# A fused attention and expert layer: the last products before routing in halves of the tokens, indexer heads in pairs, idle products, and a bank for each last quarter

## The chip, the cores and the metric

The kernel runs on one core of a Trainium2 chip. The metric is the device time of one execution in microseconds. The core has TensorE (PE, its weight loads listed apart as PEld), VectorE (DVE), ScalarE (ACT), GpSimd (POOL) and SyncE (SP), which here issues all transfers. Matrix products go to PSUM, eight banks of 128 x 512 float32; VectorE and ScalarE read them from there.

## The reference, cut to what matters

One layer on 256 tokens of width 1024, all float32:

```python
h = rmsnorm(x, g); proj = h @ w_in                     # split into latents, q/k/v, indexer q/k/w, two gates
y_a = attention(latents)  @ w_o_a                      # 8 heads, chunk-causal
score = sum_h w_i[h] * relu(q_i[h] @ k_i.T)            # indexer: 8 heads of 64, one key head
sel = top_k(score, 64)                                 # per query; attention B reads these keys alone
y_b = sparse_attention(q_b, k_b, v_b, sel) @ w_o_b
x = x + (sigmoid(g_a) * y_a + sigmoid(g_b) * y_b) @ w_out
h2 = rmsnorm(x, g2)
g_sel = argmax(h2 @ w_router_group); top 2 of the 4 experts in that group
for e in range(32):                                    # d_ff 256
    out += (silu(h2 @ w_gate[e]) * (h2 @ w_up[e])) @ w_down[e] * combine[:, e]
return rmsnorm(x + out, g_fin)
```

## The kernel before

The 256 tokens are two halves t = 0, 1 of 128. All weights stream from memory in slabs of 128 x 2048 float32 (1 MB) through SyncE's queue into a ring of 22 places; a slab's transfer is issued when the last reader of its place is done (`may_issue`, `issue`, `take`). Slabs of attention weights come first; the 96 slabs of expert weights (`w_moe`, three per expert in all: two for gate and up, and one per expert's worth of down) follow into every place that the attention stage gives up. The last three are transferred in two halves each. Places S0 and S1 hold the split parts of the last attention slabs.

Front. Products that need accuracy are done as three fp32r matmuls of high and low parts (`mm3`, lines 301 to 303: high by high, high by low, low by high). ScalarE makes the high part, VectorE the low one. Nearly all of the front is ordered by the framework's planner, which simulates a timeline. `select(j)` computes the indexer's scores for query half j: 8 heads, each a product of 64 rows (heads 0 to 3 lie in partitions 0 to 63, heads 4 to 7 in 64 to 127) with 128 key columns for j = 0 and 256 for j = 1, packed to a bank of 512 columns (`pss`, a pool of two banks), then Relu on ScalarE and a weighted sum on VectorE.

Last products. The output projection `w_out` accumulates in four banks, `acc[2*t + h]` for half t of the tokens and half h of the columns. From `raw = take()[1]` (line 872) the order on PE is written out by hand (`manual_schedule`), and from line 887 that on ScalarE and VectorE too. `last_product(t, k)` is one `mm3` of the last four slices k of column half h = 1. `added` adds the residual on VectorE, `squared` sums squares on ScalarE, `turned` transposes four blocks on PE and copies them out (`kept`), `logits` does the router's products on the turned blocks (two groups of four blocks per half of the tokens), `inv_root` makes 1/rms (square root on ScalarE, four steps on VectorE), `chosen(t)` picks group and experts in nine steps on VectorE, `cums` counts places by a product with a triangle, `place_of` and `slots` make a one-hot matrix of token to slot (`P_`) and scale it by 1/rms (`Pr`), and `gather(c, t, p)` gathers tokens for expert group 0 by products with `Pr`. `residual(i)` starts the output sums `OA` from x2 by an identity product. VectorE's work for t = 1 before is: root, choosing, then the placing of half 0, then that of half 1; the four gathers follow as (0,0), (1,0), (0,1), (1,1).

Experts. Eight groups of four experts; a group's tokens (up to 32 slots per expert) are multiplied with gate and up slabs (`gate_up`, line 993, four experts' columns of 32 side by side), folded (`hidden`, line 1009), and then with four down slabs, a quarter of the output columns each (`down`, line 1030: two halves f = 0, 1 of d_ff). `combine` evicts a result with the routing weight as high and low parts (`ysb`, line 297) and scatters it into `OA` by a product (line 1044). In groups 0 to 6 two quarters share a bank and one eviction; in the last group each quarter is evicted alone, but quarters 0 and 1, and 2 and 3, still share a bank `Y`. An engine's access to a bank is ordered behind another engine's access to the same bank, whichever columns they use. `heat(bank, n)` issues n products of 128 x 256 in bfloat16 whose result is not used. In the last group 4 of them follow each gate and up half from the second expert on. `final_part` makes x * g_fin (VectorE) and the sum of squares (ScalarE) of a finished part of the columns: 0 to 511 after quarter 2, 512 to 767 after quarter 3's eviction, and 768 to 1023 after the last scatter (line 1174 on). Then follow the root, the scaling and two output transfers.

## Time and profile before

| | us |
|---|---|
| three runs | 432.21, 435.72, 435.73 (median 435.72) |
| the profiled execution, its own time | 431.72 |
| its span, first to last instruction | 430.0 |
| TensorE busy / VectorE / ScalarE | 397.2 / 206.7 / 184.6 |
| bytes moved | 134.98 MB, 314 GB/s on the mean |

The profile is of one execution, whose time is 1.72 us above its span; it lies near the lowest of the three runs. Times in the trace count from the span's start. A matmul's row has its modelled end, so two rows overlap and the distance between starts is what a matmul takes of PE. A "releaser" (after the arrow) is what ended the idle time before an instruction.

### The profile page before, as it was taken

The page shows a single profiled execution, that of the slowest core. Times are in us where ns is not written, and L with a number is a line of the kernel's source. Part 1 is how long each engine was busy: PE and PEld are TensorE (multiplying, and loading weights), DVE is VectorE, ACT ScalarE, POOL GpSimd, SP SyncE. Part 2 cuts the span into 40 slices and gives each one's busy share as a digit, 9 for nine tenths or more (in the row PEclk, how much of TensorE's full clock was granted, in tenths as well). Part 3 has the DMA queues.
Part 4 walks back from the last instruction along what each step waited for, and adds up shares of the span by engine and source line. Part 5 has one row for each costly group of instructions (what it writes and reads, how often), then busy time and mean ns, then how long its engine had stood idle before and what let it go on. Part 6 is the DMA issues. An engine that isn't in the chain of part 4 may idle for free.

```text
span 430.0 us, 8090 instructions
## 1 busy us (share of the span) xinstructions
PE 397.2 (92%) x3255; PEld 291.6 (68%) x3255; DVE 206.7 (48%) x547; ACT 184.6 (43%) x407; POOL 26.5 (6%) x30
## 2 busy tenths in 40 slices
PE   6999999999999999999989999999999798787760
PEld 3888878888867777888877757575757374364420
DVE  2899599989757464757563221221213011020033
ACT  4885586677756566565433122212221111120242
POOL 0870000000000000000001010101010101000000
PEclk9999999999999999999999999999999979699995
DMA  7985573648543456888994999999999999999952
GB/s 261 390 357 238 196 287 111 257 171 343 197 150 143 148 204 238 325 312 335 332 356 171 425 419 418 422 419 419 420 420 421 419 419 421 421 420 418 414 215 103
DMA packets 20638, 134.98 MB, mean 314 GB/s; under 512 B 2418, under 2 KB 2930, under 8 KB 5620
## 3 DMA queue, kind: packets, MB, share of 16 engines
q1 hardware_dynamic: 20596, 134.42, 79.1%
q8 instruction: 27, 0.44, 0.4%
q14 instruction: 15, 0.12, 0.1%
HBM read 133.36 MB, written 1.05 MB: 313 GB/s over the span
## 4 chain that ended last, share of the span: by engine, by line
PE 70%; DMA 24%; DVE 2%; ACT 1%; issue 0%; SPq 0%; DVEq 0%; ACTq 0%
DMA w<-in_w_moe 23%; PE a L301 13%; PE a L302 13%; PE a L303 12%; PE G L993 8%; PE gx L844 4%; PE Y L1030 3%; PE G L1009 2%; PE OA L1044 2%; PE o L595 2%; PE s L301 2%; PE t L583 1%; PE s L303 1%; PE s L302 1%; DMA w<-in_w_att 1%; PE t L532 1%
## 5 line engine op out<-in xcount | busy, mean ns | idle before, releaser
L302 PE MATMUL a<-r 128*128 128x512 f32 (+1 forms) x244 | 93.7, 388 | 0.0
L303 PE MATMUL a<-r 128*128 128x512 f32 (+1 forms) x244 | 91.9, 383 | 0.0
L301 PE MATMUL a<-r 128*128 128x512 f32 (+1 forms) x244 | 83.7, 387 | 1.0 <-ACT r L297 1.0
L993 PE MATMUL G<-w,tok 128*32 128x256 f32 x1024 | 70.0, 401 | 13.3 <-DMA w<-in_w_moe 13.3
L297 DVE SCALAR_TENSOR_TENSOR r<-w,ident,r 128x512 fp32r<-128x512 f32 (+2 forms) x79 | 62.0, 799 | 13.5 <-ACT r L297 13.3
L297 ACT ACTIVATE r<-w,ident 128x512 fp32r<-128x512 f32 (+2 forms) x79 | 56.6, 751 | 27.4 <-PE a L303 26.2
L993 PEld LDWEIGHTS G<-w,tok 128*32 128x32 f32 x1024 | 29.6, 113 | 39.8 <-issue 15.3
L302 PEld LDWEIGHTS a<-r 128*128 128x128 f32 x244 | 45.9, 188 | 8.6 <-DVE r L297 0.4
L301 PEld LDWEIGHTS a<-r 128*128 128x128 f32 x244 | 44.8, 188 | 10.3 <-ACT r L297 1.9
L303 PEld LDWEIGHTS a<-r 128*128 128x128 f32 x244 | 45.8, 188 | 8.3
L1015 DVE TENSOR_TENSOR P<-G,P 128x64 f32<-128x64 f32 x32 | 7.2, 225 | 82.7 <-ACT P L1014 82.7
L1014 ACT ACTIVATE P<-G 128x64 f32<-128x64 f32 x32 | 7.2, 224 | 75.1 <-PE G L1009 75.1
L1030 PE MATMUL Y<-w,P 128*32 128x256 f32 x512 | 30.5, 382 | 3.2 <-DVE ysb L297 2.2
L999 ACT COPY Gs<-G 128x256 f32<-128x256 f32 x32 | 11.9, 372 | 48.0 <-PE G L993 48.0
L844 PEld LDWEIGHTS gx<-Pr,x 128*128 128x128 f32 x256 | 29.8, 195 | 3.9 <-issue 3.3
L844 PE MATMUL gx<-Pr,x 128*128 128x128 f32 x256 | 31.4, 282 | 0.5 <-DVE Pr L829 0.5
L297 DVE SCALAR_TENSOR_TENSOR ysb<-Y,ws,ysb 128x512 fp32r<-128x512 f32 (+1 forms) x18 | 12.4, 691 | 37.6 <-ACT ysb L297 20.3
L283 DVE TENSOR_TENSOR r<-w,r 128x512 fp32r<-128x512 f32 x32 | 21.9, 690 | 16.7 <-ACT r L282 15.1
L829 POOL TENSOR_SCALAR Pr<-P,r 128x128 f32<-128x128 f32 x14 | 8.3, 607 | 323.5 <-PE gx L844 198.8
L282 ACT CAST r<-w 128x512 fp32r<-128x512 f32 x32 | 19.9, 624 | 14.6 <-PE a L303 9.5
L1030 PEld LDWEIGHTS Y<-w,P 128*32 128x32 f32 x512 | 15.4, 109 | 13.7 <-DVE ysb L297 3.2
L849 DVE TENSOR_TENSOR tok<-gx,ident 128x512 f32<-128x512 f32 x16 | 11.1, 692 | 27.4 <-PE gx L844 27.3
(211 smaller groups left out, 482.2 us busy)
## 6 DMA issues: line engine op xcount, KB each, us to landing
w<-in_w_moe SPq DMA_DIRECT2D x93, 1024.0 KB, 19.8
w<-in_w_att SPq DMA_DIRECT2D x24, 1024.0 KB, 4.9
w<-in_w_moe SPq DMA_DIRECT2D x6, 512.0 KB, 15.0
w<-in_w_att SPq DMA_DIRECT2D x3, 744.0 KB, 8.5
w<-in_w_att SPq DMA_DIRECT2D x2, 512.0 KB, 5.0
out<-r SPq DMA_DIRECT2D x2, 512.0 KB, 3.8
w<-in_w_att SPq DMA_DIRECT2D x1, 768.0 KB, 4.8
w<-in_w_att SPq DMA_DIRECT2D x2, 372.0 KB, 6.1
```

The source lines that it names most:

```text
L282: nc.scalar.copy(hi, src)
L283: nc.vector.tensor_sub(lo, src, hi.bitcast(F32))
L297: return nc.scalar.mul(hi, ps, g), nc.vector.scalar_tensor_tensor(lo, ps, g, hi.bitcast(F32), op0=ALU.mult, op1=ALU.subtract)
L301: i = nc.tensor.matmul(out_, lh, rh, start=start, stop=False)
L302: nc.tensor.matmul(out_, lh, rl, start=False, stop=False)
L303: nc.tensor.matmul(out_, ll, rh, start=False, stop=stop)
L595: nc.tensor.matmul(o[r, c * 256 + 128 * b:(c + 1) * 256], v[:, b, 64 * (4 * quad + h):][:, :64], PT[:, h, 0:2] if b == 0 else PT[:, h, 2], ...
L844: nc.tensor.matmul(p[:, kk * GRP:(kk + 1) * GRP], x2[:, t, k * 128:(k + 1) * 128], Pr[:, t], start=(t == 0 and kk == 0), stop=(t == 1 and ...
L849: nc.vector.tensor_mul(tokens[c], p.rearrange("p (k s) -> p k s", k=4), bc(g_ffn[:, 4 * c:4 * c + 4], GRP, axis=2))
L993: nc.tensor.matmul(G[quarters[2 * z + o], :256], tokens[c][:, kk + o, CAP * e:CAP * e + CAP], w[:, (kk + o) * 512 + z * 256:(kk + o) * 512 ...
L999: nc.scalar.copy(Gs, G[:, :256])
L1030: nc.tensor.matmul(Y[quarters[e]], hT_[:, e, f], wv[:, f, e], start=f == 0, stop=f == 1)
```

## The change

- `select` takes heads h and h + 4 together: `mm3_pair` issues each of the three matmuls of a product for the one head and then for the other, into two banks; then both Relu and the sums follow. The order of the sum over heads changes.
- The eight last products go half by half: all four of t = 0 and then those of t = 1, with the turns and router products of both halves between them. The choosing of half 0 starts before the addition of half 1 and is completed after it. The root of half 1, the placing of half 0 (its scaled slots on POOL) and only then the choosing of half 1 follow on VectorE. Three of the four `residual` products move behind the counts, five idle products follow them, and the last count moves behind the first gather.
- `HEAT` is 5 instead of 4. In the last four `down` quarters 5 idle products stand between the halves f = 0 and f = 1 ahead of the scatter, 2 behind each quarter and 10 ahead of the last scatter.
- Each of the last four quarters has a bank of its own. The final part of columns 512 to 1023 is done in one piece after the last scatter. A scatter takes the high parts for both halves of the tokens and then the low parts, in all groups.

```diff
--- before.py
+++ after.py
@@ -23,7 +23,7 @@
 TAKEN = -3e38
 NG, EPG, NE = 8, 4, 32
 
-HEAT = 4
+HEAT = 5
 CAP = 32
 GRP = EPG * CAP
 TOPK = 64
@@ -308,6 +308,14 @@
         m = ident_r.bitcast(mybir.dt.bfloat16)
         for _ in range(n):
             nc.tensor.matmul(bank[:, 256:], m[:, :128], m, start=True, stop=True)
+
+    row_halves = slice(0, 64), slice(64, 128)
+
+    def mm3_pair(both, start, stop):
+
+        for l, r, s0, s1 in ((1, 3, start, False), (1, 4, False, False), (2, 3, False, stop)):
+            for ops in both:
+                nc.tensor.matmul(ops[0], ops[l], ops[r], start=s0, stop=s1)
 
     scr_turn = [0]
 
@@ -468,19 +476,18 @@
         per = 512 // nk
         qs = slice(j * 128, (j + 1) * 128)
         sc = e0[:, 1664:1920] if j else e0[:, 1536:1664]
-        for h0 in range(0, 8, per):
-            p = pss()
+        for h0 in range(0, 4, per):
+            p = [pss() for _ in range(2)]
             for i in range(per):
-                h = h0 + i
-                ps_ = slice(64 * (h // 4), 64 * (h // 4) + 64)
-                mm3(p[:, i * nk:(i + 1) * nk], qiT[ps_, 0, h % 4, qs], qiT[ps_, 1, h % 4, qs],
-                    kiT[ps_, 0, :nk], kiT[ps_, 1, :nk], True, True)
-            rl = wk.tile([128, 512], F32, tag="b2", name="rl", bufs=3)
-            nc.scalar.activation(rl, p, AF.Relu)
-            for i in range(per):
-                h = h0 + i
-                nc.vector.scalar_tensor_tensor(sc, rl[:, i * nk:(i + 1) * nk], wi[:, j, h:h + 1],
-                                               adm[:, 256 - nk:] if h == 0 else sc, op0=ALU.mult, op1=ALU.add)
+                mm3_pair([(p[z][:, i * nk:(i + 1) * nk], qiT[ps_, 0, h0 + i, qs], qiT[ps_, 1, h0 + i, qs],
+                           kiT[ps_, 0, :nk], kiT[ps_, 1, :nk]) for z, ps_ in enumerate(row_halves)], True, True)
+            for z in range(2):
+                rl = wk.tile([128, 512], F32, tag="b2", name="rl", bufs=3)
+                nc.scalar.activation(rl, p[z], AF.Relu)
+                for i in range(per):
+                    h = 4 * z + h0 + i
+                    nc.vector.scalar_tensor_tensor(sc, rl[:, i * nk:(i + 1) * nk], wi[:, j, h:h + 1],
+                                                   adm[:, 256 - nk:] if h == 0 else sc, op0=ALU.mult, op1=ALU.add)
         for r in range(TOPK // 8):
             m8 = wk.tile([128, 8], F32, tag="m8", name="m8")
             nc.vector.max(out=m8, in_=sc)
@@ -875,24 +882,22 @@
     def last_product(t, k):
         out_product(t, 1, 1, k, *last[k])
 
-    for k in range(2):
+    for k in range(4):
         last_product(0, k)
-        last_product(1, k)
-        turned(0, 4, k, 2)()
+        if k in (1, 2):
+            turned(0, 4, k - 1, 2)()
     logits(0, 4, 0)
-    last_product(0, 2)
-    last_product(0, 3)
+    last_product(1, 0)
     urgent = ctx.enter_context(ExitStack())
     urgent.enter_context(tc.high_priority(300))
     urgent.enter_context(tc.manual_schedule(engines={mybir.EngineType.Activation, mybir.EngineType.DVE}))
     added(512, 512, 0, acc[1])
     squared(512, 512, 0, 1)
     early = [early_root(ss2[:, t, 0:1], D, f"n2{t}") for t in range(2)]
-    last_product(1, 2)
-    last_product(1, 3)
+    last_product(1, 1)
     kept = turned(4, 4, 0, 4)
     logits(0, 4, 1)
-    added(512, 512, 1, acc[3])
+    last_product(1, 2)
     kept()
 
     def in_turn(*chains):
@@ -902,25 +907,33 @@
             chains = [c for c in chains if next(c, chains) is not chains]
 
     in_turn(inv_root(ss2[:, 0, 1:2], D, "n20", early[0], r2[:, 0:1], True))
+    logits(4, 4, 0)
+    last_product(1, 3)
+    chain = chosen(0)
+    next(chain)
+    next(chain)
+    added(512, 512, 1, acc[3])
     squared(512, 512, 1, 1)
     kept = turned(4, 4, 1, 4)
-    logits(4, 4, 0)
+    in_turn(chain)
     kept()
     cums = [pt("cum") for _ in range(2)]
-    in_turn(inv_root(ss2[:, 1, 1:2], D, "n21", early[1], r2[:, 1:2], True), chosen(0))
+
+    residual(0)
     logits(4, 4, 1)
-
-    residual(0)
-    residual(1)
     nc.tensor.matmul(cums[0][:, :NE], tri, sel[:, 0], start=True, stop=True)
     nc.tensor.matmul(cums[1][:, :NE], ones, sel[:, 0], start=True, stop=False)
+    residual(1)
     residual(2)
     residual(3)
+    heat(lgp[0], 5)
+    in_turn(inv_root(ss2[:, 1, 1:2], D, "n21", early[1], r2[:, 1:2], True))
+    place_of(0, cums[0][:, :NE])
+    in_turn(slots(0, 0, nc.gpsimd))
     in_turn(chosen(1))
-    in_turn(placed(0, cums[0][:, :NE]))
     gx = [pss("gx") for _ in range(2)]
+    gather(0, 0, gx[0])
     nc.tensor.matmul(cums[1][:, :NE], tri, sel[:, 1], start=False, stop=True)
-    gather(0, 0, gx[0])
     gather(1, 0, gx[1])
     in_turn(placed(1, cums[1][:, :NE]))
     gather(0, 1, gx[0])
@@ -1021,9 +1034,13 @@
 
     def down(grp, q, w, between=None):
 
-        if q % 2 == 0:
-            Ys[grp, q // 2] = pss("Y")
-        Y = Ys[grp, q // 2][:, 256 * (q % 2):256 * (q % 2) + 256]
+        if q % 2 == 0 or grp == NG - 1:
+            bank = pss("Y")
+            Ys[grp, q] = bank[:, :256]
+            if grp < NG - 1:
+                Ys[grp, q] = bank
+                Ys[grp, q + 1] = bank[:, 256:]
+        Y = Ys[grp, q][:, :256]
         wv = w.rearrange("p (f e c) -> p f e c", f=2, e=EPG)
         for f in range(2):
             for e in range(EPG):
@@ -1036,11 +1053,11 @@
         h, c0, w = q0 // 2, 256 * (q0 % 2), 256 * n
         pl, ws = pls[grp]
         hi, lo = (wk.tile([128, 512], F32R, tag="b2", name="ysb", bufs=3)[:, :w] for _ in range(2))
-        evac_g(hi, lo, Ys[grp, h][:, c0:c0 + w], ws)
+        evac_g(hi, lo, Ys[grp, q0][:, :w], ws)
 
         def scatter():
-            for t in range(2):
-                for v in (hi, lo):
+            for v in (hi, lo):
+                for t in range(2):
                     nc.tensor.matmul(OA[t][h][:, c0:c0 + w], pl[:, t * 128:(t + 1) * 128], v, start=False,
                                      stop=grp == NG - 1 and q0 > 0 and v is lo,
                                      skip_group_check=grp == NG - 1 and q0 == 3)
@@ -1154,29 +1171,33 @@
                 if q % 2:
                     todo.append(combine(grp, q - 1, 2))
 
-        scatter = None
+        def between():
+            heat(idle_bank, HEAT)
+            if scatter:
+                scatter()
+
+        scatter, idle_bank = None, pt("heat")
         for q in range(4):
-            down(grp, q, take()[1], scatter)
+            down(grp, q, take()[1], between)
+            heat(idle_bank, 2)
             scatter = combine(grp, q, 1)
             if q == 2:
                 for t in range(2):
                     final_part(t, 0, 512, 0)
             elif q == 3:
-                for t in range(2):
-                    final_part(t, 512, 256, 1)
-                nc.vector.tensor_add(fs[:, :, 0], fs[:, :, 0], fs[:, :, 1])
                 early = [early_root(fs[:, t, 0:1], D, f"nf{t}") for t in range(2)]
+        heat(idle_bank, 2 * HEAT)
         scatter()
 
 
     rf = sm([128, 2], "rf")
     with tc.manual_schedule(engines={mybir.EngineType.Activation, mybir.EngineType.DVE}):
-        cs = slice(768, 1024)
-        for t in range(2):
-            nc.vector.tensor_mul(ob[:, t, cs], OA[t][1][:, 256:], g_fin[0][:, cs])
+        cs = slice(512, 1024)
+        for t in range(2):
+            nc.vector.tensor_mul(ob[:, t, cs], OA[t][1], g_fin[0][:, cs])
         roots = []
         for t in range(2):
-            sumsq(OA[t][1][:, 256:], 256, fs[:, t, 2:3], scr[:, 2 * t + 1, 256:])
+            sumsq(OA[t][1], 512, fs[:, t, 2:3], scr[:, 2 * t + 1])
             roots.append(inv_root(fs[:, t, 2:3], D, f"nf{t}", early[t], rf[:, t:t + 1], True))
         for t in range(2):
             in_turn(roots[t])
```

## Rows read from the trace of the kernel before

**Rows 1.** The page: the granted clock of TensorE in 40 slices of the span, in tenths of full speed (9 is 90% or more), and from the chain that ended last its shares by engine.

```profile
PEclk9999999999999999999999999999999979699995
PE 70%; DMA 24%; DVE 2%; ACT 1%; issue 0%; SPq 0%; DVEq 0%; ACTq 0%
```

**Rows 2.** The windows view: stretch, its length, busy us (and count) of PE, PEld, DVE, ACT, POOL, then granted clock, share of the transfer engines, GB/s.

```profile
75.00:115.00 40.00, 40.00 (x229) 33.47 (x228) 36.01 (x104) 28.20 (x65) 0.00 (x0) 1.00 0.63 236
...
224.00:228.00 4.00, 3.05 (x25) 2.64 (x24) 2.98 (x21) 1.10 (x6) 0.18 (x1) 1.00 0.21 84
...
236.00:408.00 172.00, 158.44 (x1904) 102.62 (x1896) 30.68 (x87) 30.95 (x83) 7.13 (x12) 0.96 1.01 420
```

**Rows 3.** The timeline of SyncE's queue: start, duration, issues of slab transfers. No other issue lies between these two rows.

```profile
217.95 0.81 SPq L215 DMA_DIRECT2D w<-in_w_moe  x2
...
230.56 1.19 SPq L215 DMA_DIRECT2D w<-in_w_moe  x2
```

**Rows 4.** The timeline of PE in `select`: start, duration, line, result and operands, rows*columns of the weights and the moving operand's shape, count.

```profile
59.59 0.33 PE L301 MATMUL s<-r 64*128 64x128 f32 x2
...
60.21 0.27 PE L303 MATMUL s<-r 64*128 64x128 f32 x1
60.32 0.27 PE L301 MATMUL s<-r 64*128 64x128 f32 x1
...
66.19 0.28 PE L303 MATMUL s<-r 64*128 64x256 f32 x1
66.31 0.28 PE L301 MATMUL s<-r 64*128 64x256 f32 x1
```

**Rows 5.** The timeline of the last products: the first matmul of the first of the eight and the next one, the addition for half 0, and the last matmul of the last of the eight. At the end two rows of the chain that ended last (start, us on the chain): a turn and eight router products.

```profile
210.47 0.39 PE L301 MATMUL a<-r 128*128 128x512 f32 x1
...
210.69 0.39 PE L302 MATMUL a<-r 128*128 128x512 f32 x1
...
216.58 0.69 DVE L751 TENSOR_TENSOR x<-a,x 128x512 f32<-128x512 f32 x1 [1.46 <-PE a L303]
...
217.52 0.40 PE L303 MATMUL a<-r 128*128 128x512 f32 x1
...
217.92 0.44 PE t L761 x4
218.36 0.82 PE s L778 x8
```

**Rows 6.** The timeline of the routing: copy of turned blocks, two residual products, choosing for half 1 (its first step), the placing of half 0 (place, and 0.70 us later, behind the slots, the scaled slots), the four gathers, a scaling on POOL, the first expert products.

```profile
219.69 0.58 ACT L769 COPY x2T<-t 128x512 f32<-128x512 f32 x1
...
222.57 0.25 DVE L792 SCALAR_TENSOR_TENSOR lg<-s,r,b_r 128x40 f32<-128x40 f32 x1
...
223.20 1.11 PE L859 MATMUL OA<-x,ident 128*128 128x256 f32 x4
...
224.63 0.18 DVE L821 SCALAR_TENSOR_TENSOR place<-cum,sel 128x32 f32<-128x32 f32 x1
...
225.33 0.28 DVE L829 TENSOR_SCALAR Pr<-P,r 128x128 f32<-128x128 f32 x1
...
225.66 3.84 PE L844 MATMUL gx<-Pr,x 128*128 128x128 f32 x32 [0.48 <-DVE Pr L829]
...
227.82 0.61 POOL L829 TENSOR_SCALAR Pr<-P,r 128x128 f32<-128x128 f32 x1 [197.63 <-PE gx L844]
...
229.43 2.80 PE L993 MATMUL G<-w,tok 128*32 128x256 f32 x48
```

**Rows 7.** The tail. First the last slab's second half: its issue in the queue's timeline, and the transfers view of it (KB, us from issue to landing). Then the timeline: the square of columns 0 to 511, the two halves of Y of quarter 3, the last scatter, the final part of the last columns, the output transfers.

```profile
404.82 0.33 SPq L215 DMA_DIRECT2D w<-in_w_moe  x1
...
w<-in_w_moe SPq DMA_DIRECT2D x1, 512.0 KB, 11.3
...
415.50 0.59 ACT L318 ACTIVATE r<-OA 128x512 f32<-128x512 f32 x1
...
416.17 0.64 PE L1030 MATMUL Y<-w,P 128*32 128x256 f32 x8 [1.11 <-DVE ysb L297]
...
417.41 0.64 PE L1030 MATMUL Y<-w,P 128*32 128x256 f32 x8
...
419.49 0.84 PE L1044 MATMUL OA<-ysb,pl 128*128 128x256 f32 x4 [1.45 <-DVE r L1112]
...
420.03 0.42 DVE L1176 TENSOR_TENSOR r<-OA,g_fin 128x256 f32<-128x256 f32 x1
...
420.49 0.38 ACT L318 ACTIVATE r<-OA 128x256 f32<-128x256 f32 x1 [1.17 <-DVE r L1176]
...
422.61 1.57 SPq L1185 DMA_DIRECT2D out<-r  x2
```

**Rows 8.** The windows view (columns as in rows 2) of a stretch in the expert stage, of the one behind it, and of the tail; and two rows of the chain that ended last, each 16 expert products, at either clock.

```profile
339.00:342.00 3.00, 1.59 (x20) 0.80 (x20) 0.23 (x1) 0.60 (x2) 0.00 (x0) 1.00 1.00 418
342.00:345.00 3.00, 2.18 (x18) 1.00 (x18) 0.00 (x0) 0.00 (x0) 0.00 (x0) 0.53 1.03 423
...
416.00:420.00 4.00, 2.38 (x23) 1.32 (x24) 2.75 (x8) 1.96 (x9) 0.00 (x0) 1.00 0.00 0
...
300.48 1.00 PE G L993 x16
342.82 1.94 PE G L993 x16
```

## Prediction

> **What bounds the kernel now.** I read the page first. Its chain of what ended last is 70% PE and 24% waits for the expert weights [rows 1], so two regimes follow one another and must be told apart. The windows view does that. From 75 to 115 us PE has no gap while the DMA share is 0.63; from 236 to 408 us the DMA share is 1.01 at 420 GB/s and PE is not full [rows 2]. The front is bound by PE, the expert stage by the weight stream.
>
> What joins the two is the stretch in between. From 224 to 228 us the DMA share is 0.21 [rows 2]: the last places were handed out at 217.95 and the next only at 230.56, after the first expert products had consumed a slab [rows 3]. From there the stream never pauses, so **one microsecond earlier or later at the first expert product (229.43 [rows 6]) is one microsecond at the end**, whatever PE does in between. After the stream comes a tail: the last half slab lands 11.3 us after its issue at 404.82, at 416.1, and the two output transfers are issued between 422.61 and 424.18 [rows 7]. So three things can move the end: when the front is done, how long routing takes, and the tail.
>
> **Part 1, indexer heads in pairs.** Select issues 48 products of 64 rows: 24 with 128 columns, 24 with 256. One after another in the same row half they start 0.11 us apart (60.21 and 60.32) and 0.12 us apart (66.19 and 66.31) [rows 4]. Where the planner already mixed two halves, two products of 128 columns fit in 0.33 us where one alone takes 0.27 (59.59 [rows 4]), that is 0.06 us apart. Twelve of the 24 small ones stand so already (the rows marked x2 between 57.28 and 59.87); the other twelve would save 12 x 0.055 = 0.66 us. For 256 columns no row shows a pair: they save nothing if PE streams the halves one after the other, and 12 x 0.115 = 1.38 us if both run at once. I take the latter, since the nearest row, the pair of 128, halves its spacing. PE saves 2.0 us (bounds 0.66 and 2.04).
>
> The Trainium skill, "TensorE: Matmul & The Clock Gate", Part 3 (packing small matmuls), says products in different row groups run at the same time and that weight loads overlap running products only across row groups. By that the whole 2.04 us would come; by the rows alone only 0.66 us is certain. The row at 59.59 agrees as far as it goes.
>
> How much reaches the end? PE is gapless behind it [rows 2], which speaks for all; but VectorE is busy 36.01 of those 40 us, both banks must now be free together and both Relu follow the last product, and this stage's order comes from a planner that may deal it anew. Between 0 and 2.0 us, with 1 us either way for the new order, I take half: **-1.0 us** (-3.0 to +1.0).
>
> **Part 2, last products, routing and gather.** The order on PE is written out, so it can be summed. Before, the first of the last eight products starts at 210.47 and the eighth's last matmul at 217.52 [rows 5]; a product is three matmuls of 0.227 us = 0.68, a turn of four blocks 0.44, eight router products 0.82 [rows 5]. After, the first half of the tokens has its four products and two turns done at 210.47 + 4 x 0.68 + 2 x 0.44 = 214.07, 2.4 us sooner than the 216.5 that its addition at 216.58 shows. But the second half now waits behind three turns and three sets of router products: 210.47 + 8 x 0.68 + 3 x 0.44 + 3 x 0.82 = 219.69, against 217.75 before: 1.9 us later. From there:
> - addition 0.2 + 0.69, to 220.58; square and copy, 0.6 each [rows 6, 7], one after the other on ScalarE, to 221.9; router products 222.0 to 222.8.
> - The counts for the first half go behind those on PE (0.45), so its place starts at about 223.2 on VectorE, where the second root now stands ahead of it (done 223.0). Place and slots take 0.70 (224.63 to 225.33 [rows 6]): VectorE is free at 223.9. Choosing for the second half stands behind that and takes 222.57 to 224.63 = 2.06 us [rows 6]: 225.96.
> - PE meanwhile: counts, three residual products (0.55 each, from 1.11 for two), five idle ones of 256 columns (0.11 each, an estimate from the 0.12 between two fp32r products of 256 in [rows 4]; 0.55): about 225.3. The scaled slots, now on POOL at 0.61 instead of 0.28 on VectorE [rows 6], are there at 224.7, so POOL's slower form is hidden by 0.6 us; without the residuals and idle products it would cost 0.3. The first gather takes 3.84 / 4 = 0.96 [rows 6], to 226.2, and the last count queues behind it for 0.25 us.
> - Second half placed at 226.6, its slots scaled at 227.6 (0.70 + 0.33); two gathers 1.92: first expert product at **229.55**, against 229.43 to 229.50.
>
> So the later end of the second half's products (+1.9) eats what its shorter tail of work gives (-1.8): **+0.1 us**. Nine handovers between engines stand in that line, taken at 0.1 to 0.2 us each, so -1.0 to +1.5. The split places S0 and S1 are freed 1.8 us later, so two slabs are issued near 219.8 instead of 217.95; the stream has until 230.5 for them and ran dry at 224.6, so that costs nothing unless the start came over 4 us earlier.
>
> **Part 3, a bank for each last quarter.** Before, quarter 3 waits until 416.17 for VectorE to leave the bank that it shares with quarter 2 (quarter 1 with quarter 0 likewise); its end is 417.41 + 0.64 = 418.05 [rows 7]. With own banks the weights are next: the last half lands at 416.1. Five idle products and the scatter of quarter 2 stand ahead of the second half of quarter 3 on PE (0.55 + 0.45), so I get its end at 417.5 rather than at the earliest 416.8. Then 12 idle products (1.3 us) run beside the eviction of 0.48 + 0.48 us and its handovers, and reach 0.2 us past it. Scattering the high parts of both halves first leaves the first half's sum ready at 419.2, against 420.03, where the scatter had waited for a final part until 419.49 [rows 7]: -0.85. Now the final part is 512 wide in one: VectorE's product is 0.65 for 0.42 and ScalarE's square 0.59 for 0.38, one behind the other, as 420.03 and 420.49 show [rows 7]: +0.43. **Tail -0.4 us** (-1.5 to +0.5). The idle products cost nothing in the last group's gate and up work, which waits for weights.
>
> **Part 4, the idle products and the clock.** In the profiled execution they buy nothing: the granted clock is full through routing and the tail [rows 1]. But that execution is 431.72 us, one run 432.21 and two 435.72 and 435.73: two levels 3.5 us apart. A clock at half speed for a few microseconds in a stretch where PE is on the path would do that: 16 products take 1.00 us at 300.48 (2.4 GHz) and 1.94 at 342.82 (1.2 GHz), so the gather's 3.84 us would cost 3.8 more. Before that fall PE was busy 1.59 of 3 us [rows 8]; from 224 to 228 us it is busy 3.05 of 4, though with many short products [rows 2], in the tail 2.38 of 4 [rows 8], not far above. The new order fills both. I expect the upper level to go, though no row shows the clock falling there.
>
> **The sum.** -1.0 + 0.1 - 0.4 = -1.3 us against the profiled 431.72: **430.4 us**. Against the median of the runs, 435.72, that is -5.3, of which about 4 is the distance of the two levels.
>
> **Rivals.** (a) The upper level stays: its cause is not the clock, or the idle products don't reach it. Then the median is 435.72 - 1.3 = 434.4. For it: no row shows the clock falling in these places. Against it: a stretch of short bursts and gaps like theirs stands ahead of the fall at 342 us [rows 8]. (b) Routing gets later: the handovers on the second half's line cost 0.34 each instead of 0.2 (+1.3), the pairs give nothing: 431.72 + 1.4 + 0.1 = 433.2. For it: choosing the second half stands behind the placing of the first on VectorE, and the last count behind a gather on PE. Against it: the rows of the old line show less (225.33 + 0.28 to 225.66 is 0.05 [rows 6]). (c) Slower: the clock falls in the tail all the same, and the idle products, 38 of them ahead of needed work at twice 0.11 us, turn from cover into queue: a quarter then takes PE 1.9 for Y, 0.9 for its scatter and 1.5 for seven idle products, 4.3 us; four of them and the last ten idle products (2.2) end 19.4 us after the first quarter's start at 408.7, at 428.1 instead of 419.2, so 430.4 + 8.9 = 439.3. It decides at about 409 us: if the clock is half by then. Against it: it is full there now with fewer products. That the pairs change nothing is within (b).
>
> **How the numbers follow.** Forecast 0.55, with its own range 428.5 to 432; (a) 0.20; (b) 0.17; (c) 0.06; 0.02 for none of these. A change of 1%, 4.4 us, is about the least that a measurement of this kernel can tell from none. Under 431.36 lies three quarters of the forecast's chance and little of the others': faster 0.45. Above 440.1 lies not quite half of (c) and a little that I can't name: slower 0.06. The rest, 0.49, is no change. The range reaches down to the full bounds of pairs and tail (-3.0 and -1.5, not together) and up past (a) and (b): 427.6 to 435.4.
>
> **What would show it.** Pairs: products of 256 columns 0.06 apart between 57 and 74 us. Routing: first expert product within 1 us of its old distance of 19 us from the first last product (210.47 to 229.43). Tail: no wait of Y for VectorE, and 0.4 us less from the last landing to the last issue. Clock: full between 219 and 230 us and from 408 us to the last product, and runs on one level. I am wrong if the planner deals the front anew by over 2 us, or if the first expert product comes 2 us sooner, which would mean that choosing the second half does not queue as I say.

## The result, and the profile after

The median went from 434.51 us (431.5 to 436.37, 20 runs) to **431.87 us** (429.5 to 433.06, 20 runs): ratio 0.9943, 95% interval 0.9921 to 0.9965. That is 2.6 us, 0.6%: a gain, though within the 1% that the prediction took for no change, and 1.5 us above the 430.4 that was forecast. A ratio and its interval are worked out from the fast runs of both kernels, so they need not equal the quotient of two printed medians. The two profiled executions show none of it: 431.72 us before, 431.79 after, each with a span of 430.0 us. Why, the timeline tells at the first scaling of the latents, a step ahead of everything that was changed. First the kernel before, then the one after (start, duration, engine and line, operands):

```profile
27.39 0.81 DVE L495 TENSOR_SCALAR r<-a,r 128x232 f32<-128x232 f32 x2
...
211.84 0.60 PE L761 MATMUL t<-ident,x 128*128 128x128 f32 x4
...
404.85 1.07 PE L993 MATMUL G<-w,tok 128*32 128x256 f32 x16 [0.40 <-DMA w<-in_w_moe]
```

```profile
28.64 0.81 DVE L502 TENSOR_SCALAR r<-a,r 128x232 f32<-128x232 f32 x2
...
210.56 0.60 PE L768 MATMUL t<-ident,x 128*128 128x128 f32 x4
...
404.30 1.07 PE L1006 MATMUL G<-w,tok 128*32 128x256 f32 x16 [0.28 <-DMA w<-in_w_moe]
```

This execution of the kernel after began 1.25 us late for a reason that the change doesn't touch. So I read all profiles from here on by distances between five marks, taken from the timelines: the latents (the first row above), the first turn among the last products (the second row; it stands behind two of the eight products in either order), the first expert product, the last gate or up product (the last of the sixteen in the third row starts at 405.54 before and at 405.00 after), and the second output issue (423.84 and 423.88). Between the third mark and the fourth runs the weight stream, which takes 175.9 to 176.6 us in all fourteen profiles and is left out of the tables.

| kernel | latents at | latents to first turn (front) | to first expert product (routing) | last gate or up product to second output issue (tail) |
|---|---|---|---|---|
| before | 27.4 | 184.4 | 17.6 | 18.3 |
| after | 28.6 | 181.9 | 18.1 | 18.9 |

Routing and tail are each about half a microsecond longer, the front 2.5 us shorter. The page of after, by its rows on engine busy time, granted clock and the chain that ended last [rows 1]:

```profile
PE 402.6 (94%) x3304; PEld 294.5 (68%) x3304; DVE 205.6 (48%) x543; ACT 184.1 (43%) x403; POOL 28.3 (7%) x31
...
PEclk9999999999999999999999999999999789698997
...
PE 59%; DMA 37%; DVE 1%; ACT 1%; SPq 0%; issue 0%; ACTq 0%
```

More of the chain now runs over the weights (DMA 24% to 37%), and the clock's last five digits are 98997 where they were 99995: the clock stays up closer to the end.

**Front.** The timeline of `select` in after; compare [rows 4], where one product alone took 0.28 us and two starts stood 0.12 apart:

```profile
60.01 1.33 PE L318 MATMUL s<-r 64*128 64x128 f32 x20
...
65.79 0.98 PE L318 MATMUL s<-r 64*128 64x256 f32 x12
...
71.70 0.98 PE L318 MATMUL s<-r 64*128 64x256 f32 x12
```

Twelve products of 256 columns fit in 0.98 us. With 0.28 for the last, the other eleven starts are (0.98 - 0.28)/11 = 0.064 us apart on the mean. For 128 columns it is (1.33 - 0.27)/19 = 0.056. The trace has them start in twos: the two products of a pair stand at most 0.005 us apart, and the next two 0.11 to 0.12 us later (0.16 and 0.22 behind the first two of a stretch of 128 and of 256 columns). So two products of different row halves run at once. Counted from each stretch's start to the start of what PE did next, the 48 products took 5.76 us before and 3.45 us after: **2.3 us less**.

**Routing.** The timeline of after [rows 5, 6]: first of the eight products, the last matmul of them, the addition for half 1, placing for half 0, choosing for half 1, idle products, gathers, first expert products.

```profile
209.19 0.39 PE L301 MATMUL a<-r 128*128 128x512 f32 x1
...
218.49 0.39 PE L303 MATMUL a<-r 128*128 128x512 f32 x1
218.91 0.69 DVE L758 TENSOR_TENSOR x<-a,x 128x512 f32<-128x512 f32 x1 [0.31 <-PE a L303]
...
222.33 0.19 DVE L828 SCALAR_TENSOR_TENSOR place<-cum,sel 128x32 f32<-128x32 f32 x1 [0.52 <-PE cum L924]
...
222.83 0.25 DVE L799 SCALAR_TENSOR_TENSOR lg<-s,r,b_r 128x40 f32<-128x40 f32 x1
...
223.73 0.71 PE L310 MATMUL s<-ident_r 128*128 128x256 bf16 x5
224.27 1.06 PE L851 MATMUL gx<-Pr,x 128*128 128x128 f32 x8
...
226.66 2.05 PE L851 MATMUL gx<-Pr,x 128*128 128x128 f32 x16 [0.17 <-DVE Pr L836]
...
228.64 2.80 PE L1006 MATMUL G<-w,tok 128*32 128x256 f32 x48
```

The last two gathers (16 products) wait for the slots of half 1 (the bracket at 226.66, 0.17 us): choosing for half 1, with the placing behind it, ends last.

**Tail.** Issue and landing of the last half slab in the queue's timeline and the transfers view, then the timeline of after [rows 7]:

```profile
404.28 0.33 SPq L215 DMA_DIRECT2D w<-in_w_moe  x1
...
w<-in_w_moe SPq DMA_DIRECT2D x1, 512.0 KB, 11.3
...
415.45 0.64 PE L1047 MATMUL Y<-w,P 128*32 128x256 f32 x8
416.02 0.72 PE L310 MATMUL heat<-ident_r 128*128 128x256 bf16 x5
416.50 0.72 PE L1061 MATMUL OA<-ysb,pl 128*128 128x256 f32 x4
417.15 0.64 PE L1047 MATMUL Y<-w,P 128*32 128x256 f32 x8
417.72 1.48 PE L310 MATMUL heat<-ident_r 128*128 128x256 bf16 x12
418.96 0.71 PE L1061 MATMUL OA<-ysb,pl 128*128 128x256 f32 x4
419.59 1.29 DVE L1197 TENSOR_TENSOR r<-OA,g_fin 128x512 f32<-128x512 f32 x2 [0.25 <-PE OA L1061]
...
422.77 1.46 SPq L1206 DMA_DIRECT2D out<-r  x2
```

Y of quarter 3 waits for VectorE no longer. But its last weights are there at 404.28 + 11.3 = 415.6 and its last half starts at 417.15, and after it PE has no gap up to the last scatter. The wait has become a queue.

### The profile page after: what moved, and what is told of

Read it like the earlier page. It is cut to its first block, busy times and chain, and to the rows that moved or that the text cites. A ratio compares the mean times of both kernels' runs of the same rounds, so it can differ in the third digit from the quotient of the medians.

```text
span 430.0 us, 8183 instructions
## 1 busy us (share of the span) xinstructions
PE 402.6 (94%) x3304; PEld 294.5 (68%) x3304; DVE 205.6 (48%) x543; ACT 184.1 (43%) x403; POOL 28.3 (7%) x31
## 4 chain that ended last, share of the span: by engine, by line
PE 59%; DMA 37%; DVE 1%; ACT 1%; SPq 0%; issue 0%; ACTq 0%
DMA w<-in_w_moe 35%; PE a L301 13%; PE a L302 13%; PE a L303 13%; PE G L1006 3%; PE gx L851 2%; PE o L602 2%; PE Y L1047 2%; PE t L590 1%; DMA w<-in_w_att 1%; PE heat L310 1%; PE s L301 1%; PE s L302 1%; PE s L303 1%; PE s L785 1%; PE t L539 1%
## 5 line engine op out<-in xcount | busy, mean ns | idle before, releaser
L1006 PE MATMUL G<-w,tok 128*32 128x256 f32 x1024 | 71.4, 407 | 10.3 <-DMA w<-in_w_moe 10.1
L297 DVE SCALAR_TENSOR_TENSOR r<-w,ident,r 128x512 fp32r<-128x512 f32 (+2 forms) x79 | 62.0, 799 | 12.8 <-ACT r L297 12.4
L301 PEld LDWEIGHTS a<-r 128*128 128x128 f32 x244 | 45.2, 190 | 11.3 <-ACT r L297 2.6
L297 DVE SCALAR_TENSOR_TENSOR ysb<-Y,ws,ysb 128x512 fp32r<-128x512 f32 (+1 forms) x18 | 12.4, 691 | 39.3 <-ACT ysb L297 20.6
L1022 PEld LDWEIGHTS G<-cst,Gs 128*128 128x128 f32 x128 | 17.5, 199 | 9.9 <-issue 5.6
## 6 DMA issues: line engine op xcount, KB each, us to landing
w<-in_w_moe SPq DMA_DIRECT2D x93, 1024.0 KB, 19.8
```

Of the source, the lines that this page charges most:

```text
L297: return nc.scalar.mul(hi, ps, g), nc.vector.scalar_tensor_tensor(lo, ps, g, hi.bitcast(F32), op0=ALU.mult, op1=ALU.subtract)
L301: i = nc.tensor.matmul(out_, lh, rh, start=start, stop=False)
L1006: nc.tensor.matmul(G[quarters[2 * z + o], :256], tokens[c][:, kk + o, CAP * e:CAP * e + CAP], w[:, (kk + o) * 512 + z * 256:(kk + o) * 512 ...
L1022: nc.tensor.matmul(HT[:, f * 64:(f + 1) * 64], Gs[:, f * 128:(f + 1) * 128], fold, start=True, stop=True)
```

## The experiments

The theory was the prediction's: pairs give about 1 us, banks 0.4, and idle products hold the clock. The rivals: idle products do nothing or cost, and all comes from pairs and banks. The comparisons that follow are with before runs on the same chip; there the median of before was 435.01, 434.59 and 434.68 us in the three groups.

**Before again** (e1_before_again): the kernel before, with no edit.

> The kernel before, unchanged, to see what differs between its own executions, which spread from 431.5 to 436.4 us. Theory C (the clock): in the long executions the clock stands at half in routing or in the tail, so a longer execution has a lower mean clock; about 0.4% less mean clock for 3.5 us more. Rival D (the stream): the mean clock does not go with the time, and the spread comes from when the weights arrive. Both expect a ratio of 1.00.

434.84 us (432.23 to 437.02), ratio 0.9996 [0.9973, 1.002]. Not two levels but a spread of 5 us. Against the first profile of before, this one is late in two places. The windows of this run [columns as in rows 2], and one of the first before for the same stretch:

```profile
8.00:12.00 4.00, 2.86 (x10) 2.58 (x11) 1.96 (x3) 2.37 (x4) 0.00 (x0) 0.62 1.01 409
...
224.00:228.00 4.00, 2.63 (x14) 2.02 (x13) 3.55 (x23) 0.00 (x0) 0.00 (x0) 0.93 0.62 258
228.00:232.00 4.00, 4.00 (x25) 4.00 (x25) 1.43 (x11) 1.10 (x6) 0.60 (x1) 0.64 0.01 2
```

```profile
8.00:12.00 4.00, 3.38 (x21) 2.89 (x22) 3.14 (x4) 2.78 (x5) 0.00 (x0) 1.00 1.03 414
```

At the start the clock is at 0.62 on average where the other execution had full speed, and the latents stand at 30.0 instead of 27.4. And in routing it falls to half, so that the gather is stretched and the first expert product is late:

```profile
227.41 5.47 PE L844 MATMUL gx<-Pr,x 128*128 128x128 f32 x32 [0.48 <-DVE Pr L829]
...
232.80 2.80 PE L993 MATMUL G<-w,tok 128*32 128x256 f32 x48
```

5.47 us for 3.84, and routing as a whole 19.2 for 17.6.

Of the two theories in the expectation, the mean clock supports the first weakly. Over the 91 executions of before in the three groups (e1's twelve among them), a lower mean clock goes with a longer time (correlation -0.45), by 0.13 us for each 0.001 of full speed. So 0.4% less clock goes with 0.5 us, not with 3.5. The mean counts every stretch alike, also those in which PE waits for weights, so it says little on routing and tail.

**All idle products alone** (e2_idle_alone), in the banks of before:

```diff
-HEAT = 4
+HEAT = 5
...
     residual(3)
+    heat(lgp[0], 5)
...
-        scatter = None
+        def between():
+            heat(idle_bank, HEAT)
+            if scatter:
+                scatter()
+        scatter, idle_bank = None, pt("heat")
         for q in range(4):
-            down(grp, q, take()[1], scatter)
+            down(grp, q, take()[1], between)
+            heat(idle_bank, 2)
...
+        heat(idle_bank, 2 * HEAT)
         scatter()
```

> The kernel before with the idle products of the change alone (5 for 4 in the last group, 5 in routing, and those of the last four quarters, there in the old shared banks). Theory C: most of the 2.6 us of the change comes with them, 432 us, and the spread shrinks to 430.5 to 433. Rival D: nothing or a loss of up to 1 us from the idle products that stand ahead of needed ones in the tail, 434.5 to 435.5, with the old spread.

434.97 us (433.1 to 436.93), ratio 1.0008 [0.9984, 1.0031]. The upper end of the spread is still there. Routing is at full clock (17.6), but the tail takes 20.4 us instead of 18.3. Its timeline:

```profile
419.57 1.48 PE L310 MATMUL heat<-ident_r 128*128 128x256 bf16 x12
421.08 0.84 PE L1045 MATMUL OA<-ysb,pl 128*128 128x256 f32 x4
```

The last scatter starts when the twelve idle products have passed. The median shows at most 1.4 us of those 2.1 (the interval's upper end).

**Pairs alone** (e3_pairs_alone, and again as e9_pairs_again):

```diff
+    def mm3_pair(both, start, stop):
+        for l, r, s0, s1 in ((1, 3, start, False), (1, 4, False, False), (2, 3, False, stop)):
+            for ops in both:
+                nc.tensor.matmul(ops[0], ops[l], ops[r], start=s0, stop=s1)
...
-        for h0 in range(0, 8, per):
-            p = pss()
+        for h0 in range(0, 4, per):
+            p = [pss() for _ in range(2)]
```

> The kernel before with the indexer's heads in pairs alone. In the profiles the first of the last products stands 1.3 us earlier after the change (209.19 for 210.47). If that is the pairs' doing, this kernel has it too and is 1.3 us shorter than the kernel before, 433.2 us, with the first expert product 1.3 us earlier. If the planner dealt it, any value between -1 and +1.5 us may come. Theory C expects the spread of the kernel before to stay.

> The kernel before with the heads in pairs alone, once more, since the first time gave 4 us where the products' own saving on PE is 2.0 us and the front of its profile is 2.4 us shorter. If the pairs are worth 2.4 us and the rest was chance, 432 us; if they are worth 4, 430.9.

First 430.94 us, ratio 0.9909 [0.9886, 0.9932]; then 431.64, ratio 0.9944 [0.991, 0.9979]. The intervals overlap from 0.991 to 0.9932, some 3 to 4 us. The front takes 182.0 and 180.9 us, where the latents stand at 27.4 and 30.6; before it was 184.4 from 27.4, in e1 183.6 from 30.0. At like starts that is 2.5 and 2.6 us less. In the second profile the tail took 19.8 us, with the clock at half in it:

```profile
416.00:418.00 2.00, 2.00 (x16) 1.13 (x12) 1.04 (x2) 0.30 (x2) 0.00 (x0) 0.50 0.00 0
418.00:420.00 2.00, 0.77 (x8) 0.00 (x0) 0.66 (x2) 1.16 (x5) 0.00 (x0) 0.50 0.00 0
```

**Heads in turn, in two banks** (e10_serial_heads): pairs alone, but `mm3_pair` issues one head's three matmuls, then the other's.

```diff
-        for l, r, s0, s1 in ((1, 3, start, False), (1, 4, False, False), (2, 3, False, stop)):
-            for ops in both:
+        for ops in both:
+            for l, r, s0, s1 in ((1, 3, start, False), (1, 4, False, False), (2, 3, False, stop)):
```

> The pairs' two banks, the same order of heads, Relu and sums, but with a head's three products issued together and the other head's three behind them, as far as the planner leaves them so. If the gain is that two row halves stream at the same time, it goes for the products of 256 columns: they stand 0.12 us apart again, and of the 2.4 us at least 1.4 are lost, 433 to 434 us. If the gain is the planner's new order around two banks, it stays: 431 to 432.

430.79 us, ratio 0.9941 [0.9904, 0.9979], front 181.1: as with pairs. It was meant to keep the two halves from running at once, and didn't, as the timeline shows:

```profile
66.00 0.98 PE L318 MATMUL s<-r 64*128 64x256 f32 x12
```

Twelve in 0.98 us again. The planner isn't what mixes them: in the program that this kernel builds to, the heads stand in turn, three products of one and then three of the other (only the first product of 128 columns is split up). Yet the trace has the twelve start in twos, 0.009 to 0.011 us apart, with 0.106 to 0.110 from one two to the next (0.21 behind the first). So here PE starts a product of the other row half without waiting for the two that are written between. What before lacked is neighbours: its program has all heads of one row half ahead of those of the other, and only products where the two meet overlap (the rows marked x2 [rows 4]). So products of the two halves need to stand within a few places of each other; issuing them alternately, as `mm3_pair` does, adds nothing that the front shows.

**The change without pairs** (e11_no_pairs): its `select` is that of before.

```diff
-        for h0 in range(0, 4, per):
-            p = [pss() for _ in range(2)]
+        for h0 in range(0, 8, per):
+            p = pss()
```

> The changed kernel with the heads as before, one after the other. If the pairs carry the change, the rest is worth nothing or a loss: 434 to 435 us, the front 2.4 us longer from the first latents to the first turn. If the pairs' 4 us were chance, 433.

434.07 us, ratio 1.0002 [0.9972, 1.0032]; front 184.1. The other three parts together gain nothing: by the profile they cost 1.1 us (routing 0.5, tail 0.6), which the interval, 1.2 us less to 1.4 more, leaves open.

**The new order alone** (e8_order_alone): before, with the second block of the diff (last products, routing, gather, five idle products).

```diff
-    for k in range(2):
+    for k in range(4):
         last_product(0, k)
-        last_product(1, k)
-        turned(0, 4, k, 2)()
+        if k in (1, 2):
+            turned(0, 4, k - 1, 2)()
```

> The kernel before with the new order of the last products, routing and gather alone, its five idle products included. My sum: +0.1 us where the clock is full. Theory C adds -1 to -2 us on the median for a clock that no longer falls, so 433 to 434; rival E expects 434.5 to 435.4.

434.63 us, ratio 1.0002 [0.9975, 1.0029]. Routing takes 18.1 us instead of 17.6.

**Five idle products in the routing alone** (e5_routing_idle):

```diff
     residual(3)
+    heat(lgp[0], 5)
```

> The kernel before with five idle products in routing alone (behind the fourth residual product, in the old order). A profile of the kernel before shows the clock at half from about 227 to 231 us and a first expert product 5.4 us after the first gather instead of 3.7. Theory C: the idle products keep the clock up, so this kernel is 1 to 2 us shorter than the kernel before, and its profile has the clock full from 220 to 236 us. Rival E: routing's clock is a matter of a few executions; then nothing moves, 434.5 to 435.2.

433.74 us, ratio 0.9975 [0.9946, 1.0005]: a gain that can't be told from none. Routing 17.6 at full clock; but in the tail the clock fell, and the tail took 19.6:

```profile
410.00:412.00 2.00, 0.98 (x9) 0.22 (x9) 0.48 (x1) 0.45 (x1) 0.00 (x0) 0.79 1.02 408
412.00:414.00 2.00, 2.00 (x17) 1.32 (x20) 0.00 (x0) 0.00 (x0) 0.00 (x0) 0.50 0.71 287
```

**The change without idle products** (e4_no_idle):

```diff
-HEAT = 5
+HEAT = 4
...
-    heat(lgp[0], 5)
...
-            down(grp, q, take()[1], between)
-            heat(idle_bank, 2)
+            down(grp, q, take()[1], scatter)
...
-        heat(idle_bank, 2 * HEAT)
```

> The changed kernel without any of its added idle products (4 for 5 in the last group, none in routing, none in the last four quarters). Theory C: it falls back by 2 us or more to 434, with long executions up to 436. Rival D: it stays at 431.9 or gains up to 0.7 us, since the tail loses 12 idle products that stood ahead of the last scatter (0.2 us past the eviction) and 5 ahead of each second half.

**429.68 us** (428.2 to 430.47), ratio 0.9866 [0.9843, 0.9889]: faster than the change (0.9921 to 0.9965), whose best run (429.5) is about this one's median. There are only five runs of it. Routing 18.1, tail 17.2.

**Without those of the last four quarters alone** (e6_no_tail_idle): as e4, but `HEAT` stays 5 and the five in the routing stay.

```diff
-            down(grp, q, take()[1], between)
-            heat(idle_bank, 2)
+            down(grp, q, take()[1], scatter)
...
-        heat(idle_bank, 2 * HEAT)
```

> The changed kernel without the idle products of the last four quarters, but with those in routing and 5 for 4 in the last group. If the 2.2 us between the changed kernel and the one without idle products are all in the tail, this is 429.7 too. If the routing's idle products also cost, it lies between, near 430.3; if they earn 1 to 2 us (theory C), it is the shortest, 428 to 429.

430.06 us, ratio 0.9899 [0.9858, 0.9939]; routing 18.1, tail **17.2** where the change takes 18.9. Its timeline against that of after:

```profile
415.45 0.64 PE L1047 MATMUL Y<-w,P 128*32 128x256 f32 x8 [0.63 <-DMA w<-in_w_moe]
416.02 0.74 PE L1061 MATMUL OA<-ysb,pl 128*128 128x256 f32 x4
416.68 0.64 PE L1047 MATMUL Y<-w,P 128*32 128x256 f32 x8
417.92 1.02 PE L1061 MATMUL OA<-ysb,pl 128*128 128x256 f32 x4 [0.59 <-ACT ysb L297]
418.86 1.29 DVE L1190 TENSOR_TENSOR r<-OA,g_fin 128x512 f32<-128x512 f32 x2
...
422.04 1.46 SPq L1199 DMA_DIRECT2D out<-r  x2
```

The idle products of the expert stage (`HEAT`) and of the routing, which e6 has and e4 has not, show neither in the distances nor, within the intervals, in the times. Y waits for its weights, the last scatter for the eviction (the bracket), and neither for PE. The scatter starts 417.92 - 416.68 = 1.24 us after the last half of Y; in after it is 418.96 - 417.15 = 1.81. Part of that comes back, since e6's scatter waits within for the low parts: from the last half of Y to the final part it is 418.86 - 416.68 = 2.18 in e6 and 419.59 - 417.15 = 2.44 in after.

**That with the old order** (e7_old_order): e6, with last products, routing and gather as before, and five idle products behind `residual(3)`.

```diff
-    for k in range(4):
+    for k in range(2):
         last_product(0, k)
-        if k in (1, 2):
-            turned(0, 4, k - 1, 2)()
+        last_product(1, k)
+        turned(0, 4, k, 2)()
```

> As the one before it, but with the old order of the last products and of routing (five idle products behind the fourth residual product). My sum for the new order was +0.1 us; in the profiles the new order takes 18.0 and 18.1 us from the first turn to the first expert product, the old one 17.6 where its clock is full. If that is so on the mean, this kernel is 0.4 us shorter than the one before it; if the new order's gain is a full clock that the old order cannot keep even with idle products, it is 1 us longer.

430.02 us, ratio 0.9892 [0.9853, 0.9932]: as e6 (430.06), though its routing is 17.6.

**Pairs and banks, nothing else** (e12_pairs_banks): e4 with the old order, so no added idle product either.

```diff
-            down(grp, q, take()[1], between)
-            heat(idle_bank, 2)
+            down(grp, q, take()[1], scatter)
...
-    heat(lgp[0], 5)
```

> Only what has paid so far: pairs and a bank for each last quarter with its final part and scatter order; the old order of routing, and no added idle product. The pairs' 2.4 to 4 us and the banks' 1.3 to 1.7 us (the tail from the first down product to the last issue, 15.1 us before and 14.0 in the kernel without tail idle products) make 428.5 to 430.5 us, shorter than the change by 2 us. Theory C expects it longer than the version with five idle products in routing (430.0) by up to 1 us.

**429.01 us** (427.49 to 431.21), ratio 0.9896 [0.9865, 0.9928]. Its span is the shortest that was profiled, 426.9 us, with the last outputs issued at

```profile
419.80 1.46 SPq L1193 DMA_DIRECT2D out<-r  x2
```

instead of 422.77 in after. With e4 it has the lowest times of all, and the two can't be told apart (their intervals overlap). Both beat the kernel before. Against the change, e4's interval lies clear below; that of e12 touches it (0.9928 against 0.9921).

All distances together, read as in the small table above:

| kernel | latents at | front | routing | tail |
|---|---|---|---|---|
| e1 before | 30.0 | 183.6 | 19.2 (clock falls) | 18.3 |
| e2 all idle products | 27.8 | 183.6 | 17.6 | 20.4 |
| e5 idle in routing | 27.6 | 184.4 | 17.6 | 19.6 (clock falls) |
| e8 new order | 26.8 | 184.5 | 18.1 | 18.3 |
| e11 change without pairs | 27.0 | 184.1 | 18.1 | 18.9 |
| e3 pairs | 27.4 | 182.0 | 17.6 | 18.4 |
| e9 pairs | 30.6 | 180.9 | 17.6 | 19.8 (clock falls) |
| e10 pairs, heads in turn | 29.7 | 181.1 | 17.6 | 18.3 |
| e4 change without idle | 30.5 | 181.0 | 18.1 | 17.2 |
| e6 without idle in the tail | 30.9 | 180.9 | 18.1 | 17.2 |
| e7 e6 in the old order | 31.0 | 180.9 | 17.6 | 17.2 |
| e12 pairs and banks | 29.1 | 181.1 | 17.6 | 17.2 |

## Why the prediction was right, and where it was not

The sum was -1.3 us. The distances give -2.3 (pairs) + 0.5 (order) - 1.1 (banks, with scatter and final part) + 1.7 (idle products in the tail) = **-1.2 us**. But no term is the one that I wrote: the sum came out because the errors cancelled, which is luck. The median of 431.87 lies just inside the forecast's 428.5 to 432. Part by part:

**Part 1 was less than half of what came.** Forecast -1.0 of 2.04 us saved on PE, since I let VectorE and a new order of the planner take half. The saving on PE was sized well: 2.3 us measured, with 0.064 us for the 0.06 that I took between two of 256 columns and 0.056 for the small ones. I put the overlap that was there before down to the planner; as e10 shows, PE does it by itself where the two halves meet. What failed is the step to the end: every kernel with pairs has a front of 180.9 to 182.0 us, every one without 183.6 to 184.5. A straight line through the fourteen fronts against their starts puts the pairs at -2.3 us (standard error 0.2), with 0.3 us less front for each microsecond of later start. So all of the 2.3 us that PE saves arrives. The row to rely on was the first of [rows 2]: with PE gapless for 40 us what it saves is saved, and VectorE's 36.01 of 40 us left room for it.

The Trainium skill ("TensorE: Matmul & The Clock Gate", Part 3) says that small matmuls in different row groups run at the same time. The trace bears it out: the products of a pair start at most 0.005 us apart, where products of 256 columns in one row half needed 0.12 us each.

**Part 2 was right on the queue and 0.4 us short in size.** Forecast +0.1, measured +0.5 in after, e4, e6, e8 and e11 (18.1) against all with the old order at full clock (17.6). I had the last of the eight products 1.9 us later; from the first product it was 218.49 - 209.19 = 9.30 us against 217.52 - 210.47 = 7.05, so 2.25 later. Those 0.3 us were there at the addition already, and the long line of handovers behind it, of which I had been most afraid, added the last 0.1. Choosing for half 1 does stand behind the placing of half 0 (222.33, then 222.83). POOL's slower scaling is hidden as forecast: the first gather starts at 224.27, right behind the five idle products, and the last two still wait for half 1. No measured time shows the 0.5, though: e6 and e7 are equal, e4 and e12 within their intervals, and e8 equals before; each of these comparisons leaves a microsecond or more open. Nothing came of doing one half first, and what rival (b) feared came to 0.4 us of its 1.3. (Its sum counts the 0.1 twice and leaves out the tail's -0.4; by its own terms it gives 432.7, not 433.2.)

**Part 3 had the right direction and went wrong by the company it was in.** Forecast -0.4, with the idle products counted at 0.55 ahead of the last half of Y and 0.2 behind it; measured -1.1 without them (e4, e6, e7, e12: 17.2 against 18.3) and +0.6 with them. No run takes the own banks, the scatter order and the final part in one piece apart, but the stretches of the tail do:

| kernel | last landing to last half of Y | to the final part | to the second output issue |
|---|---|---|---|
| before | 1.3 | 2.6 | 3.8 |
| e6 (e4, e7 and e12 alike) | 0.1 | 2.2 | 4.3 |
| after | 1.6 | 2.4 | 4.3 |

The bank is worth 1.1 us. The scatter, which takes the high parts first and no longer waits for a final part, brings 0.4, and the final part in one piece costs 0.5, close to the 0.43 that I had. The step that failed is the end of the last half of Y, which I had 1.4 us behind the landing (417.5 against 416.1): in after it is 417.15 + 0.64 - 415.6 = 2.2. I costed the five idle products ahead of that half, at 0.55, and not what the earlier ones do: in after the first halves of Y start at 408.16, 410.28, 412.87 and 415.45, the last three without a wait for weights:

```profile
408.16 0.64 PE L1047 MATMUL Y<-w,P 128*32 128x256 f32 x8 [0.74 <-DMA w<-in_w_moe]
...
410.28 0.64 PE L1047 MATMUL Y<-w,P 128*32 128x256 f32 x8
...
412.87 0.64 PE L1047 MATMUL Y<-w,P 128*32 128x256 f32 x8
```

A quarter takes PE 2.58 us with its seven idle products, which is about the pace of the weights; so when the last half lands at 415.6, 1.6 us of queue lie ahead of it, where e6 has 0.1. The twelve idle products behind it cost less, 0.3 us up to the final part, close to the 0.2 that I had. This is rival (c)'s queue at a full clock: 1.7 us instead of 9.

**Part 4 was half right.** I took four runs for two levels; twenty show one spread (431.5 to 436.37), and e2, with every idle product, has it as well (433.1 to 436.93). So the upper level did not go because of them. Half-clock stretches in routing and tail do exist in some executions of the old layout and cost time in the way the mechanism said, if less than the 3.8 us that I gave a gather at half clock throughout: 1.6 us in the routing (e1), 1.3 to 1.5 in the tail (e5, e9). The idle products may well cover those: e2's median shows at most 1.4 of the 2.1 us that they add to its tail. No run shows it directly. But in the tail of the change they charge 1.7 us for it, more than such a fall costs; and e4 and e12, which add none, never came above 430.47 and 431.21. Rival (a), the upper level that stays, was thus nearer on the cause, though not on the time. Whether the five in the routing are worth anything stays open: e5's interval ends just past 1.

**Against the medians.** I forecast -5.3 from the 435.72 of three runs; from the 434.51 of twenty it was -2.6 (interval 1.5 to 3.4). The terms explain 1.2 of it. An excess stands in some of the others too: the terms give -2.9 for e4 and -3.4 for e12, measured were 5.8 (4.8 to 6.8) and 4.5 (3.1 to 5.9) less. In e12, as in e6, e7, e9 and e10, the interval still holds the sum; in the change, e3 and e4 it doesn't. What could fill it are executions of the kernel before in which the clock falls in routing or tail (1.3 to 1.6 us each): they are in its median, and none of the four profiles with banks of their own and no idle products in the tail shows one there. One profile of a kernel can't weigh how often it happens, so this stays open.

## What to carry to other kernels

Where the trace shows an engine without a gap, count the whole of what is taken off it; discount only where a second engine is shown busier. Small products of different row halves should stand side by side in the program. Products that are only there to keep a clock up are a queue like any other: place them where the trace shows a wait that is longer than they are, and don't count on a wait that the same change removes. Before comparing two single profiles, find the first mark that the change can't reach and take its offset off.

## What the runs showed of the hardware

PE starts a product of one row half ahead of products of the other half that are written before it: in e10 the starts of two such products stand 0.009 to 0.011 us apart, though the program has two others between them.

The clock's first rise to full came between 5.6 and 14.3 us after the start in these profiles (7.69 before, 11.73 after, 14.32 in e6), with the same code in front. The latents stood at 26.8 to 27.8 us where it rose by 8.5, and at 28.6 to 31.0 where it rose at 11.7 or later; e1 (30.0) had it at 5.6, but at half again from 9.0 to 12.4. That is up to 4 us between executions, more than the whole effect of the change. The Trainium skill ("TensorE: Matmul & The Clock Gate", Part 1) says that the first cold stretch differs from run to run and costs under 1% of a typical span. The trace agrees on the first; on the second, the differences between executions alone are 4 of 430 us, 0.9%, and no run here starts at full clock, so the whole cost isn't measured.

Also not expected: the clock's fall in the routing (e1) or in the tail (e5, e9) comes in some executions and not in others, with the same instructions there.
